# A bound moved behind its exponential, from VectorE to GpSimd, in the time mixing of an RWKV-7 trunk

## The chip, the cores and the metric

The kernel runs on one core of one Trainium2 chip. The metric is the device time of one execution in microseconds. The engines are named as the profile names them: PE is TensorE's matmuls and PEld its weight loads, DVE is VectorE, ACT is ScalarE, POOL is GpSimd, SP is SyncE, which issues most DMAs. An engine works through its own queue in order; the engines wait for each other by semaphores.

## The reference, cut to what matters

Two layers work on 256 tokens of width 2048. The first layer is RWKV-7 time mixing and an MLP, the second chunked attention and an MLP. The change is in the time mixing, where two low-rank products give a decay and a rate for each token and channel:

```python
w_log = -jax.nn.softplus(-(w0 + jnp.tanh(xw @ w1) @ w2)) - 0.5
a = jax.nn.sigmoid(a0 + (xa @ a1) @ a2)
...
decay = jnp.exp(-jnp.exp(heads(w_log)))
...
S = (S * w_t[:, :, None, :] + sa[..., None] * (kk_t * a_t)[:, :, None, :]
     + v_t[..., None] * k_t[:, :, None, :])
```

With z the sum in the inner brackets, softplus(-z) is ln(1 + exp(-z)), and the sigmoid of z is exp(-ln(1 + exp(-z))). Both halves share the inner exponential and the logarithm.

## The kernel before, in words

The 32 heads are worked as 16 pairs of 64 + 64 channels, one pair to the 128 partitions, with the 256 tokens along the free dimension. The recurrence is replaced by four chunks of 64 tokens: inside a chunk a triangular matrix is inverted by products, and the state is carried from chunk to chunk.

The work on a pair is a generator of 36 steps in three parts: early (8 steps), invert (12) and late (16). A new pair begins every 8 slots, so up to five pairs are under way at a time. When one pair takes its first early step, the pair ahead takes its first invert step and the one before that the ninth invert step.

A slot is put together thus. First come the small products of the pairs under way, inversions before the rest, in an order that the program fixes on PE. Behind them come twelve dense products of a projection (w_k, then w_r, for the pair that begins next), which fill PE while the other engines prepare the following slot. Weight halves are made at given places of the eight slots: wH by ACT (L420), wL by DVE (L423). DVE also adds up the modulation, one 128x1024 block at a time (L501). The order of a queue on ACT, DVE and POOL is otherwise set by a planner when the program is built. It goes by program order and by what it reckons to be ready first. A change of an instruction or of its engine can therefore move other instructions too.

These are the steps that the change and the prediction speak of:

- early, step 1: the two low-rank products z on PE (L157, L158) into one PSUM bank of 512 columns (two such banks, "ms", go round), the bound (L162, DVE), the exponential (L163, ACT), and the split square of k (L145, L148 on ACT, L149 on DVE).
- early, step 2: the logarithm (L167) and the two outer exponentials (L168, L169) on ACT.
- early, steps 3 to 6: the running sum of the log decay (L174, DVE), its exponentials (L176, L178, ACT), and on POOL pc (L180), km (L188), bh (L190, L201) and kh (L205).
- invert, step 1: ar (L246, DVE) and the diagonal blocks da and co (L252, L254, ACT) out of one product. Then POOL makes u (L255, L256) and the masks al (L259).
- invert, further steps: u is turned by DVE (L266, the tile tt), PE multiplies it with al (L135), ACT copies the product (xs, L278 and L283), PE multiplies again, DVE adds to u (L289). In the ninth invert step and behind it POOL copies u into uf (L284).
- late: chunk by chunk on PE (L588), with ACT's g and sa (L324, L330), DVE's zs (L341, L343) and ACT's zd (L349); at the end the variance's pair of activations (L358, L359).

The tile that takes the bound is one [128, 512] buffer, "s2", used by every pair in turn: the decay's half is sw, the rate's half is a.

Of the kernel before, what the change touches and what calls it, by code (L numbers as in the profile page):

```python
# [14 lines left out]
AF = mybir.ActivationFunctionType  # L15
ALU = mybir.AluOpType
# [61 lines left out]
class Pair:  # L78
# [13 lines left out]
    def s(self, name="s", bufs=6):  # L92
        return self.b.pw.tile([P, T], F32, tag=name, bufs=bufs, name=name)
# [4 lines left out]
    @staticmethod  # L98
    def ch(t):
        return t.rearrange("p (c t) -> p c t", t=C)  # L100
# [51 lines left out]
    def early(self):  # L152
        b, nc, j, v, s, ch = self.b, self.b.nc, self.j, self.v, self.s, self.ch
        pw, vec, cst, e01 = b.pw, b.vec, b.cst, self.e01
        lw = self.lw
        z = b.psm()
        nc.tensor.matmul(z[:, 0:T], lw[:, 0, :], self.tw, start=True, stop=True)  # L157
        nc.tensor.matmul(z[:, T:2 * T], lw[:, 1, :], self.ta, start=True, stop=True)  # L158

        both = pw.tile([P, 2 * T], F32, tag="s2", bufs=1, name="s2")  # L160
        sw, a = both[:, 0:T], both[:, T:2 * T]
        nc.vector.tensor_scalar(out=both, in0=z, scalar1=-80.0, scalar2=None, op0=ALU.max)  # L162
        nc.scalar.activation(both, both, AF.Exp, scale=-1.0)  # L163
        k = self.k
        sq = self.parts(k, None, AF.Square, vec("k_k", j))
        yield
        nc.scalar.activation(both, both, AF.Ln, bias=b.col(C_ONE))  # L167
        nc.scalar.activation(sw, sw, AF.Exp, scale=-1.0, bias=b.col(C_MHALF))  # L168
        nc.scalar.activation(a, a, AF.Exp, scale=-1.0)  # L169
        yield  # L170
        pss = b.psm()[:, :T]
        self.head_sums(pss, sq)
        cum = s()
        nc.vector.tensor_tensor_scan(out=cum, data0=cst("reset"), data1=sw, initial=0.0, op0=ALU.mult, op1=ALU.add)  # L174
        e0, e1 = e01[:, :, 0:C], e01[:, :, 1:C + 1]
        nc.scalar.activation(e1, ch(cum), AF.Exp, scale=-1.0)  # L176
        e2 = s()
        nc.scalar.activation(e2, cum, AF.Exp)  # L178
        self.pc = pw.tile([P, 4, 1], F32, tag="pc", bufs=4, name="pc")
        nc.gpsimd.tensor_copy(self.pc, e01[:, :, C:C + 1])  # L180
        yield
        rs, ss, rr = s(), s(), s()
        nc.vector.tensor_scalar(out=ss, in0=pss, scalar1=1e-24, scalar2=None, op0=ALU.max)
        nc.scalar.activation(rs, ss, AF.Ln)
        nc.scalar.activation(rs, rs, AF.Exp, scale=-0.5)
        nc.scalar.activation(rr, rs, AF.Square)
        km = s()
        nc.gpsimd.tensor_scalar(out=km, in0=a, scalar1=-1.0, scalar2=vec("k_a", j), op0=ALU.add, op1=ALU.mult)  # L188
        self.bh, self.kh = s("bh", 1), s("kh", 2)
        nc.gpsimd.tensor_tensor(out=self.bh, in0=a, in1=e2, op=ALU.mult)  # L190
        yield
        nc.vector.scalar_tensor_tensor(out=rr, in0=rr, scalar=-0.5, in1=ss, op0=ALU.mult, op1=ALU.mult)
        nc.vector.scalar_tensor_tensor(out=rs, in0=rr, scalar=1.5, in1=rs, op0=ALU.add, op1=ALU.mult)
        kk = s()
        nc.vector.scalar_tensor_tensor(out=kk, in0=k, scalar=vec("k_k", j), in1=rs, op0=ALU.mult, op1=ALU.mult)
        nc.vector.scalar_tensor_tensor(out=km, in0=km, scalar=1.0, in1=k, op0=ALU.add, op1=ALU.mult)
        yield
        r, kr = self.r, self.big("kr", 4)
        self.kr = kr
        nc.vector.tensor_tensor(out=kr[:, :, 0:C], in0=ch(kk), in1=e0, op=ALU.mult)  # L200
        nc.gpsimd.tensor_tensor(out=self.bh, in0=self.bh, in1=kk, op=ALU.mult)  # L201
        nc.vector.tensor_tensor(out=kr[:, :, C:P], in0=ch(r), in1=e1, op=ALU.mult)
        rkp = s()
        nc.vector.scalar_tensor_tensor(out=rkp, in0=r, scalar=vec("r_k", j), in1=km, op0=ALU.mult, op1=ALU.mult)
        nc.gpsimd.tensor_tensor(out=self.kh, in0=km, in1=e2, op=ALU.mult)  # L205
        rkp = self.parts(rkp, rkp)
        yield

        self.vp = pw.tile([P, 4, C], F32, tag="vp", bufs=4, name="vp")
        pt = self.two()  # L210
        yield self.each(pt, 0, C, lambda c: ch(v)[:, c, :], lambda c: cst("cen"))
        nc.scalar.copy(self.even_odd(self.vp), self.by_chunk(pt, 2, C))
        yield
        pt = self.two()
        bk = self.bk = b.pw.tile([P, 3, 2, C], F32, tag="bk", bufs=4, name="bk")
        yield [p for i, t in enumerate((self.bh, self.kh))
               for p in self.each(pt, 2 * C * i, C, lambda c: ch(t)[:, c, :], lambda c: self.b.cst("eye"), 3)]
        for e in range(2):
            p_ = pt[:, e, 0:4 * C].rearrange("p (a i k) -> p i a k", a=2, k=C)
            nc.scalar.copy(bk[:, e::2], p_[:, 0:2 - e])  # L220
        pbn = b.psm()[:, :T]
        self.head_sums(pbn, rkp)
        nc.vector.tensor_tensor(out=v, in0=pbn, in1=v, op=ALU.mult)
        yield
# [145 lines left out]
class Body:  # L370
# [9 lines left out]
    def cst(self, name, rows=slice(None)):  # L380
        o, n = CST_AT[name]
        return self.csts[rows, o:o + n]
# [5 lines left out]
    def vec(self, name, kt=None):  # L388
        i = VI[name]
        return self.vecs[:, i, :] if kt is None else self.vecs[:, i, kt:kt + 1]  # L390
# [1031 lines left out]
```

## Time and profile before

| | us |
|---|---|
| median of 3 runs | 2601.4 (2600.03 to 2603.03) |
| profiled execution | 2600.04 |
| its span | 2598.3 |
| stretch in which pairs 2 to 15 are worked | about 225 to 575 |

The page of the profile gives the busy time of each engine over the span. A view by stretches of time gives the same for a part of it. A view of the waits lists who waited for whom. The timeline lists instructions in order of time: start in us from the span's start, duration in us, engine, line, operation, what it writes and reads, its shape, how often; in square brackets stands the idle time of the engine in front of it and who ended it. The ends of matmuls are modelled, so a busy PE may still hold short gaps.

### The profile page before, as it was taken

The numbers are of one execution on the slowest core, as the hardware profiler recorded it, in microseconds if no ns is written. First come the engines' busy times: TensorE is split into PE (matmuls) and PEld (weight loads), VectorE is DVE, ScalarE is ACT, GpSimd is POOL, SyncE is SP. The second block draws the span as 40 slices with busy tenths as digits, with TensorE's granted clock in tenths as the row PEclk, the third lists the DMA queues.
The fourth block names the chain that finished last, engine by engine and source line by source line (L and its number), as shares of the span: only waits on it lengthen the run. The fifth ranks groups of instructions, "written<-read, shape, count | busy, mean of one in ns | idle before, by whom it ended". The sixth has DMA issues, their size and how long they took to land.

```text
span 2598.3 us, 58875 instructions
## 1 busy us (share of the span) xinstructions
PE 2541.2 (98%) x24018; PEld 2225.7 (86%) x24018; DVE 2075.9 (80%) x3020; ACT 1371.4 (53%) x2535; POOL 229.2 (9%) x336
## 2 busy tenths in 40 slices
PE   6998999999999999999999999999999999999998
PEld 4788888888998888888888988887998888888887
DVE  6888889998899888888889898899896555556555
ACT  3346666674565364464455554565564463553554
POOL 0003333331200000000001000000100000000001
PEclk9999999999999999999999999999999999999999
DMA  9966666667869899888898688887676555555553
GB/s 364 366 232 195 216 213 223 212 217 222 307 220 338 322 329 343 326 323 316 313 323 291 201 305 304 309 277 261 233 258 212 187 187 188 187 188 191 187 187 130
DMA packets 207119, 662.65 MB, mean 255 GB/s; under 512 B 21248, under 2 KB 53632, under 8 KB 206848
## 3 DMA queue, kind: packets, MB, share of 16 engines
q1 hardware_dynamic: 205072, 657.02, 73.1%
q8 instruction: 188, 3.08, 0.5%
q10 hardware_dynamic: 1776, 1.87, 0.2%
q14 instruction: 83, 0.68, 0.1%
HBM read 656.71 MB, written 2.10 MB: 254 GB/s over the span
## 4 chain that ended last, share of the span: by engine, by line
PE 80%; DVE 10%; issue 4%; ACT 3%; DMA 2%; POOL 1%; SPq 0%; ACTq 0%; DVEq 0%; POOLq 0%
PE pj L454 43%; PE pj L456 21%; DVE acc L501 3%; PE pj L443 3%; PE pj L444 2%; PE pj L445 2%; DVE wL L423 2%; PE lt L588 1%; PE o L443 1%; DMA rada<-w_ada 1%; ACT wH L420 1%; PE o L444 1%; PE o L445 1%; ACT da L252 1%; PE pT L1310 0%
## 5 line engine op out<-in xcount | busy, mean ns | idle before, releaser
L423 DVE TENSOR_TENSOR wL<-raw,wH 128x1024 fp32r<-128x1024 f32 x771 | 946.6, 1229 | 336.7 <-ACT wH L420 334.1
L420 ACT CAST wH<-raw 128x1024 fp32r<-128x1024 f32 x771 | 805.3, 1045 | 729.6 <-PE pj L454 579.0
L454 PE MATMUL pj<-aHL,wH 128*128 128x512 f32 x2816 | 894.0, 398 | 1.2 <-DVE x L1135 1.1
L454 PE MATMUL pj<-hHL,wH 128*128 128x512 f32 x2048 | 644.2, 396 | 0.0
L456 PEld LDWEIGHTS pj<-aHL,wL 128*128 128x128 f32 x2816 | 531.7, 189 | 124.2 <-issue 0.3
L456 PE MATMUL pj<-aHL,wL 128*128 128x256 f32 x2816 | 563.0, 281 | 0.0
L501 DVE SCALAR_TENSOR_TENSOR acc<-rada,ct,acc 128x1024 f32<-128x1024 f32 x360 | 462.7, 1285 | 9.5 <-DMA rada<-w_ada 9.1
L456 PEld LDWEIGHTS pj<-hHL,wL 128*128 128x128 f32 x2048 | 384.2, 188 | 91.1 <-DVE wL L423 0.7
L454 PEld LDWEIGHTS pj<-aHL,wH 128*128 128x128 f32 x2816 | 431.6, 189 | 8.9 <-issue 8.5
L456 PE MATMUL pj<-hHL,wL 128*128 128x256 f32 x2048 | 402.0, 278 | 0.3 <-DVE wL L423 0.3
L454 PEld LDWEIGHTS pj<-hHL,wH 128*128 128x128 f32 x2048 | 312.0, 189 | 1.3 <-DVE hHL L1181 1.1
L443 PE MATMUL pj<-aHL,wH 128*128 128x256 f32 (+1 forms) x896 | 263.4, 294 | 1.5 <-ACT r L1018 1.4
L444 PE MATMUL pj<-aHL,wH 128*128 128x256 f32 (+1 forms) x896 | 253.7, 283 | 0.0
L445 PE MATMUL pj<-aHL,wL 128*128 128x256 f32 (+1 forms) x896 | 252.5, 282 | 0.0
L620 POOL TENSOR_TENSOR ss<-ss,sq 128x256 f32<-128x256 f32 x56 | 52.7, 942 | 1579.7 <-ACT sq L619 1532.1
L443 PEld LDWEIGHTS pj<-aHL,wH 128*128 128x128 f32 x896 | 169.8, 189 | 6.1 <-ACT r L1018 2.1
L1206 DVE SCALAR_TENSOR_TENSOR x<-pj,mod,x 128x256 f32<-128x256 f32 x256 | 123.4, 482 | 64.1 <-PE pj L456 61.1
L444 PEld LDWEIGHTS pj<-aHL,wH 128*128 128x128 f32 x896 | 169.6, 189 | 0.8
L445 PEld LDWEIGHTS pj<-aHL,wL 128*128 128x128 f32 x896 | 170.1, 190 | 0.2
L1178 ACT ACTIVATE t<-t 128x256 f32<-128x256 f32 x112 | 46.8, 418 | 119.6 <-DVE t L1150 119.6
L1181 DVE TENSOR_TENSOR hHL<-t,hHL 128x256 fp32r<-128x256 f32 x128 | 53.9, 421 | 1.8 <-ACT t L1180 1.1
L1180 ACT ACTIVATE t<-t 128x256 f32<-128x256 f32 x128 | 53.3, 416 | 3.3
(270 smaller groups left out, 2757.9 us busy)
## 6 DMA issues: line engine op xcount, KB each, us to landing
rada<-w_ada SPq DMA_DIRECT2D x320, 512.0 KB, 5.2
raw<-w_up SPq DMA_DIRECT2D x256, 512.0 KB, 4.1
raw<-w_down SPq DMA_DIRECT2D x256, 512.0 KB, 3.8
rada<-w_ada_kv SPq DMA_DIRECT2D x64, 512.0 KB, 6.3
rawa<-w_ada SPq DMA_DIRECT2D x32, 512.0 KB, 9.1
rawa<-w_ada_t SPq DMA_DIRECT2D x32, 512.0 KB, 8.6
raw<-w_k SPq DMA_DIRECT2D x32, 512.0 KB, 5.0
raw<-w_r SPq DMA_DIRECT2D x32, 512.0 KB, 4.0
```

The source lines that it names most:

```text
L420: nc.scalar.copy(Hf, raw)
L423: eng.tensor_tensor(out=Lf, in0=raw, in1=Hf, op=ALU.subtract)
L443: nc.tensor.matmul(ps, H[:, i, :], a(kt)[:, 0, :], start=(first and kt == 0), stop=False)
L444: nc.tensor.matmul(ps, H[:, i, :], a(kt)[:, 1, :], start=False, stop=False)
L445: ins = nc.tensor.matmul(ps, L[:, i, :], a(kt)[:, 0, :], start=False, stop=(last and kt == KT - 1))
L454: nc.tensor.matmul(ps, w[kt // HK][0][:, kt % HK, :], a(kt), start=(kt == 0), stop=False)
L456: ins = nc.tensor.matmul(ps[:, 0, :], w[kt // HK][1][:, kt % HK, :], a(kt)[:, 0, :], start=False, stop=(kt == KT - 1))
L501: nc.vector.scalar_tensor_tensor(out=self.acc, in0=raw, scalar=ck, in1=self.acc, op0=ALU.mult, op1=ALU.add)
L620: (eng or nc.gpsimd).tensor_tensor(out=self.ss, in0=self.ss, in1=sq, op=ALU.add)
L1180: nc.scalar.activation(t, t, AF.Square)
L1181: nc.vector.tensor_tensor(out=h[:, 1, :], in0=t, in1=h[:, 0, :], op=ALU.subtract)
L1206: nc.vector.scalar_tensor_tensor(out=x, in0=ps[:, i, :], scalar=self.mods[(layer, 5)][:, n:n + 1], in1=x, op0=ALU.mult, op1=ALU.add)
```

## The change

The maximum with -80 by DVE, which read the product out of PSUM and wrote the tile, is removed. ACT's exponential now reads PSUM itself and writes the tile. Behind it POOL takes the minimum with exp(80) in place, and the logarithm reads what POOL left. The value that the logarithm sees is the same up to rounding: exp(-max(z, -80)) is min(exp(-z), exp(80)).

```diff
         both = pw.tile([P, 2 * T], F32, tag="s2", bufs=1, name="s2")
         sw, a = both[:, 0:T], both[:, T:2 * T]
-        nc.vector.tensor_scalar(out=both, in0=z, scalar1=-80.0, scalar2=None, op0=ALU.max)
-        nc.scalar.activation(both, both, AF.Exp, scale=-1.0)
+        nc.scalar.activation(both, z, AF.Exp, scale=-1.0)
+        nc.gpsimd.tensor_scalar(out=both, in0=both, scalar1=math.exp(80.0), scalar2=None, op0=ALU.min)
         k = self.k
         sq = self.parts(k, None, AF.Square, vec("k_k", j))
         yield
```

## The prediction

> **What bounds the kernel now.** I read the page first, then the busy times of the stretch in which the sixteen head pairs are worked (225 to 575 us), then the waits there, then one pair in order of time.
>
> ```profile
> span 2598.3 us, 58875 instructions
> ...
> PE 2541.2 (98%) x24018; PEld 2225.7 (86%) x24018; DVE 2075.9 (80%) x3020; ACT 1371.4 (53%) x2535; POOL 229.2 (9%) x336
> ```
>
> TensorE is busy nearly throughout. The same in the pairs' stretch (start and end, its length, then busy us of PE, PEld, DVE, ACT, POOL, the granted clock, the DMA share and GB/s):
>
> ```profile
> 225.00:575.00 350.00, 337.96 (x8183) 305.44 (x8184) 318.38 (x558) 225.02 (x651) 130.13 (x162) 1.00 0.67 217
> ```
>
> PE is at 97% (338.0 of 350), DVE at 91%, ACT at 64%, POOL at 37%, at the full clock. So what is taken from DVE counts only where PE waits for it. The waits from 225 to 600 us (who waits, for whom: us in total, times, longest):
>
> ```profile
> POOL kh L205 <- DVE s L196: 35.7, 15, 3.4
> ...
> DVE tt L266 <- POOL u L256: 7.5, 12, 1.0
> ...
> ACT da L252 <- DVE ar L246: 6.9, 11, 1.1
> ...
> DVE u L289 <- PE iv L135: 4.1, 8, 1.1
> ...
> PE iv L135 <- DVE tt L266: 3.4, 7, 1.2
> PE iv L135 <- issue: 2.9, 5, 0.8
> ...
> PE iv L135 <- POOL al L259: 2.3, 3, 0.9
> ```
>
> PE's three longest sums are 3.4, 2.9 and 2.3 us, 8.6 us together, or 0.3% of the span. That is about all this stretch has to give. Now one pair, the eighth, around the changed lines (start, duration, engine, line, operation):
>
> ```profile
> 369.22 1.04 ACT L420 CAST wH<-raw 128x1024 fp32r<-128x1024 f32 x1
> 369.49 0.59 PE L158 MATMUL ms<-ta,lw 128*128 128x256 f32 x2
> ...
> 370.24 0.42 DVE L246 TENSOR_TENSOR ar<-gr,csts 128x256 f32<-128x256 f32 x1
> ...
> 370.75 0.26 ACT L252 COPY da<-gr 32x128 f32<-32x128 f32 x1 [0.48 <-DVE ar L246]
> ...
> 370.91 0.68 DVE L162 TENSOR_SCALAR s<-ms 128x512 f32<-128x512 f32 x1
> ...
> 371.96 0.29 DVE L289 TENSOR_TENSOR u<-u,iv 128x128 f32<-128x128 f32 x1 [0.37 <-PE iv L135]
> ...
> 372.18 0.63 ACT L163 ACTIVATE s<-s 128x512 f32<-128x512 f32 x1
> ...
> 372.23 0.41 POOL L255 TENSOR_TENSOR u<-da,csts 128x128 f32<-128x128 f32 x1 [14.10 <-ACT da L252]
> ...
> 372.72 0.41 POOL L256 TENSOR_TENSOR u<-u,csts 128x128 f32<-128x128 f32 x1
> ...
> 372.84 0.73 ACT L167 ACTIVATE s<-s,csts 128x512 f32<-128x512 f32 x1
> ...
> 373.08 1.11 POOL L259 TENSOR_TENSOR al<-da,csts 128x512 f32<-128x512 f32 x1
> ...
> 373.16 0.32 DVE L266 STREAM_TRANSPOSE tt<-u 128x128 f32<-128x128 f32 x1 [0.57 <-POOL u L256]
> ...
> 373.56 1.72 DVE L423 TENSOR_TENSOR wL<-raw,wH 128x1024 fp32r<-128x1024 f32 x1
> ...
> 374.13 2.52 POOL L284 COPY uf<-u 32x128 f32<-32x128 f32 x2
> ...
> 374.43 0.23 PE L135 MATMUL iv<-tt,al 32*32 32x32 f32 x3
> ```
>
> Two things are to be seen. The urgent chain is ar (L246), da (ACT), u and al (POOL), then PE's product of tt and al: al ends at 374.19 and PE starts on it at 374.43, 0.24 us of slack. And the removed bound (L162) lies beside this chain, in front of a gap: DVE then waits 0.37 us for PE and 0.57 us for POOL.
>
> **The change, part by part.** These are the rows for the prices (min, median, max in ns):
>
> ```profile
> L162 DVE TENSOR_SCALAR s<-ms x16: 683/684/692, 203.5 to 575.9; 128x512 f32<-128x512 f32 x16
> L163 ACT ACTIVATE s<-s x16: 614/632/635, 204.3 to 577.2; 128x512 f32<-128x512 f32 x16
> L188 POOL TENSOR_SCALAR s<-s,vecs x16: 476/646/1749, 210.0 to 584.9; 128x256 f32<-128x256 f32 x16
> L180 POOL COPY pc<-e x16: 186/644/1059, 209.0 to 583.8; 128x4 f32<-128x4 f32 x16
> L259 POOL TENSOR_TENSOR al<-da,csts x16: 1087/1107/1121, 224.4 to 603.8; 128x512 f32<-128x512 f32 x16
> L145 ACT ACTIVATE sq<-s x16: 416/417/419, 215.5 to 593.8; 128x256 fp32r<-128x256 f32 x16
> L145 ACT ACTIVATE sq<-lt x16: 383/384/387, 288.2 to 656.9; 128x256 fp32r<-128x256 f32 x16
> ```
>
> *Removed from DVE:* 16 x 0.684 = 10.9 us. No DMA moves. Behind L162 come DVE's waits for PE (4.1 us in all) and for POOL's u (7.5 us), 11.6 us together, as much as is removed: most of it only lengthens them. Bounds: nothing, if the gap swallows all, and 3.4 us, if PE's waits for the transposes (L266) all go. I take 1.5 us gained, near the middle, because two transposes run per step and only one of them can come earlier; the other waits for POOL.
>
> *ScalarE reads PSUM:* the same 512 columns. L145 takes 417 ns out of SBUF and 384 out of PSUM, so I expect 0.63 - 0.03 = 0.60 us, 16 x 0.03 = 0.5 us in all, off the urgent chain: nothing. The bank of the product is released when the exponential ends instead of the maximum; if ScalarE keeps its place that is 372.81 instead of 371.59, 1.2 us later, and the other "ms" bank serves meanwhile. Without that cover PE would wait up to 1.2 us per pair, 19 us; I take nothing, as PE's listed waits show none on an "ms" bank being full.
>
> *Place of the exponential:* it no longer needs L162, so it is ready when L158 ends (about 370.1), and ScalarE is idle from 370.26 to 370.75, before da. This idle time is 6.9 us over 11 pairs. The exponential can go there, or stay behind da. In front, 16 x 0.60 = 9.6 us stand against 6.9, so da comes up to 2.7 us late in sum, some 0.17 us per pair, against 0.24 us of slack of al: bounds 0 and 2.7 us lost. I take 0.5, nearer to nothing because of that slack. It costs the whole 0.60 us per pair, 9.6, where ScalarE has no idle time there.
>
> *Added on POOL:* no row shows a one-input operation on 512 columns there. Undisturbed, L188 takes 476 ns for 256 columns and L180 186 for 4, so (476 - 186) / 252 = 1.15 ns a column and 476 + 256 x 1.15 = 771 ns (estimate). Below it stands 476, the half size; above it 1107, two inputs of 512 columns; L188's slowest (1749) adds 1.27 for a disturbed one: 2.04. I take 0.8 us; POOL is at 37%, and with 16 x 0.8 = 12.8 us in the stretch stays near 41%.
>
> *The new wait:* the logarithm (L167) waits for POOL. Behind it on ScalarE stand both exponentials, the variance's pair (L358, L359) and the copies xs and g that PE needs. With the exponential ahead of da it ends near 370.9, the minimum by 371.7, before da ends at 372.15: POOL is free then (idle 14.10 us before L255) and the logarithm can start when it does now. Behind da, the minimum follows al (374.19) and ends at 375.0; the logarithm is 2.1 us later, and the planner can put other work of ScalarE ahead of it. On POOL the copies uf (L284) and km (L188) come up to 0.8 us later; behind km POOL waits 35.7 / 15 = 2.4 us per pair for DVE (L205), which covers it. I take nothing, bounds under the rivals.
>
> *Sum:* -1.5 + 0.5 = -1.0 us on the profiled execution's 2600.0 us (the span of 2598.3 and 1.7 around it), 2599.0. The median of the three runs shown is 1.4 us above the profiled time, so I forecast 2600.4.
>
> *The shared read path.* POOL and DVE disturb each other here: L423 took 1.72 us beside al and uf, against its mean in the whole kernel:
>
> ```profile
> L423 DVE TENSOR_TENSOR wL<-raw,wH 128x1024 fp32r<-128x1024 f32 x771 | 946.6, 1229 | 336.7 <-ACT wH L420 334.1
> ```
>
> That is 0.49 us more. The Trainium skill ("SBUF — State Buffer", section "Who interferes with whom") says that a VectorE instruction with two SBUF inputs and a GpSimd instruction that reads SBUF contend for one read interface, and that the later one blocks fully. By that rule the work moved to POOL would take from DVE as much as it frees. In this trace the delay is part of the POOL work beside it, so the rule is half borne out; I take it as the second rival below.
>
> **The rivals.**
>
> 1. *The relief reaches PE.* Both transposes come earlier, and the exponential leaves ScalarE's chain. For it speaks the chain of waits one pair later, which runs through it to the variance's exponential:
>
> ```profile
> 397.64 0.64 ACT s L163
> ...
> 400.65 0.42 ACT sl L359
> ```
>
> PE's waits for the transposes (3.4) and al (2.3) and half of those put down to issue (1.45) go: 7.2 us gained, 2594.2. Against it: al is on POOL and is not sped up.
>
> 2. *DVE gets nothing.* The minimum holds up L423 or the modulation's L501 (both read two SBUF inputs) for its 0.77 us: 16 x 0.77 = 12.3 us against 10.9 freed. The gain of 1.5 drops out and 1.4 us of DVE work are added: +1.4 + 0.5 = 1.9, 2603.3. For it L423's 1.72; against it DVE's gap at 371.6 to 371.96, where the minimum would lie.
>
> 3. *The minimum gets in front of al.* POOL works in order; a minimum between L256 and L259 makes al late by 0.8 to 1.1 us, less 0.24 of slack: 0.56 to 0.86 us of PE per pair, times 15 (the first pair has no second inversion beside it) 8.4 to 12.9, middle 10.7: 2612.1, slower. It decides as soon as the minimum begins behind 372.2 and ahead of al. Against it: al stands earlier in the program and is ready when u is.
>
> 4. *ScalarE stalls.* The logarithm waits 2.1 us behind al with the order of ScalarE's queue kept. The next copy that PE needs:
>
> ```profile
> 376.18 0.27 ACT L278 COPY xs<-iv 128x128 f32<-128x128 f32 x1
> ```
>
> ```profile
> 377.19 0.23 PE L135 MATMUL iv<-u,xs 32*32 32x32 f32 x3
> ```
>
> It ends at 376.45, 0.74 us ahead of PE; 2.1 - 0.74 = 1.36 us per pair, times 13, is 17.7 us: 2619.1. Against it: the planner sets the queue's order, and the exponential fits ahead of da.
>
> If the planner moved nothing but left the exponential behind da with other work filling the wait, the change would in effect do nothing; that lies inside the first forecast.
>
> **How the numbers follow.** The forecast (2600.4) has a chance of 0.36, rival 1 0.29, rival 2 0.09, rival 3 0.12, rival 4 0.14. I count 0.2%, 5.2 us, as what a measurement here tells from no change. Rival 1 is faster (0.29), the forecast and rival 2 are the same (0.45), rivals 3 and 4 slower (0.26). The range reaches below rival 1 to 2592, as all 8.6 us of PE's three waits could go (2592.8), and above to the middle of rival 3 (2612): outside lie rival 4 and half of rival 3's upper part. The likeliest case's own range, from -3.4 to +2.7 us, is 2598 to 2604.
>
> **What would show it.** Right: L162 gone from DVE; the exponential's start ahead of da or next to it; a POOL row of 0.7 to 1.1 us for the minimum; DVE's waits for L289 and u grown by most of 10.9 us; al's end unmoved against PE's product; PE busy within 2 us in the stretch. Rival 1: PE's wait for the transposes near nothing. Rival 2: the L423 beside the minimum at 1.7 us or more while others stay near 1229 ns, and DVE no less busy in the stretch than 318.4 us. Rival 3: PE's wait for al well above 2.3 us. Rival 4: ScalarE waiting for POOL ahead of L167 by 2 us. The forecast is wrong if PE's idle time in the stretch changes by over 5 us.

## The result, and the profile after

The changed kernel is slower: a median of 2647.9 us in 5 runs (2645.9 to 2648.3) against 2601.4, a ratio of 1.0169 [1.0157, 1.018] (the brackets hold a 95% interval), or 44 us by the ratio; the two medians are 46.5 us apart, the spans of the two profiled executions 46.1. The forecast was 2600.4. In the profiled execution (2646.2 us) two lines of the page show nearly the same instructions, busy a little longer:

```profile
span 2644.4 us, 58878 instructions
...
PE 2557.9 (97%) x24018; PEld 2239.8 (85%) x24018; DVE 2071.0 (78%) x3004; ACT 1369.8 (52%) x2535; POOL 236.2 (9%) x352
```

DVE has its 16 instructions fewer and POOL its 16 more. The loss lies in the pairs' stretch. The view by stretches, with the columns of the row of before (busy us of PE, PEld, DVE, ACT, POOL, granted clock, DMA share, GB/s):

```profile
225.00:575.00 350.00, 316.53 (x7255) 284.79 (x7257) 280.82 (x489) 200.56 (x581) 123.41 (x162) 0.95 0.60 197
```

PE is idle 33.5 us of the 350, where it was idle 12.0, and its granted clock is 0.95, where it was 1.00. In the same time it does 7255 products instead of 8183. The two changed lines (duration min, median and max in ns, then the first and the last start in us):

```profile
L162 ACT ACTIVATE s<-ms x16: 596/597/602, 203.1 to 618.2; 128x512 f32<-128x512 f32 x16
...
L163 POOL TENSOR_SCALAR s<-s x16: 1486/2339/2377, 203.8 to 621.1; 128x512 f32<-128x512 f32 x16
```

L162 is now the exponential and L163 the minimum. The exponential of the first and of the last pair are 415.1 us apart; before they were 372.9 (204.3 to 577.2). So 15 intervals grew by 42.2 us, 2.8 us each, which is nearly the whole of the 46.1 us between the two spans. The exponential costs 0.60 us, as worked out; the minimum costs 2.34 and not 0.77. Who waits for whom from 225 to 640 us (us in total, times, longest):

```profile
ACT s L167 <- POOL s L163: 54.7, 15, 4.3
...
PE ms L135 <- ACT xs L283: 23.0, 11, 2.8
...
DVE u L289 <- PE iv L135: 12.5, 14, 1.7
...
PE ms L523 <- ACT xs L283: 4.3, 2, 2.2
```

The first row leads to the second and the fourth: the logarithm (L167) waits 54.7 us for the minimum, and PE waits 23.0 + 4.3 = 27.3 us in 13 pairs for a copy (xs, L283) that ACT has standing behind the logarithm. None of the three was among the waits of this stretch before. The eighth pair in order of time:

```profile
382.71 0.59 PE L158 MATMUL ms<-ta,lw 128*128 128x256 f32 x2
...
383.91 0.26 ACT L252 COPY da<-gr 32x128 f32<-32x128 f32 x1 [0.42 <-DVE ar L246]
...
385.34 0.60 ACT L162 ACTIVATE s<-ms 128x512 f32<-128x512 f32 x1
...
386.26 1.12 POOL L259 TENSOR_TENSOR al<-da,csts 128x512 f32<-128x512 f32 x1
...
386.73 1.72 DVE L423 TENSOR_TENSOR wL<-raw,wH 128x1024 fp32r<-128x1024 f32 x1
...
387.46 2.34 POOL L163 TENSOR_SCALAR s<-s 128x512 f32<-128x512 f32 x1
...
388.38 1.62 DVE L501 SCALAR_TENSOR_TENSOR acc<-rada,ct,acc 128x1024 f32<-128x1024 f32 x1
...
389.84 0.72 ACT L167 ACTIVATE s<-s,csts 128x512 f32<-128x512 f32 x1 [3.90 <-POOL s L163]
...
391.89 0.53 ACT L283 COPY xs<-ms 32x128 f32<-32x128 f32 x2
...
392.46 0.44 PE L135 MATMUL ms<-u,xs 32*32 32x32 f32 x16 [2.13 <-ACT xs L283]
```

To compare with before, put both kernels on PE's time: L158 began at 369.49 and now begins at 382.71, 13.22 us later. The exponential stayed behind da, where it was (372.18 + 13.22 = 385.40, now 385.34). al ends at 387.38, or 374.16 on the old time; it was 374.19. The minimum begins directly behind al and ends at 389.80. The logarithm, at 372.84 + 13.22 = 386.06 before, now starts at 389.84, 3.78 us late. ACT makes up part of that, because the copy xs now ends 2.58 us behind the logarithm's start (392.42 - 389.84). It was 3.32 us before, when PE began its product 0.87 us behind the end of xs (376.16 to 377.03):

```profile
375.63 0.53 ACT L283 COPY xs<-ms 32x128 f32<-32x128 f32 x2
...
377.03 0.34 PE L135 MATMUL ms<-u,xs 32*32 32x32 f32 x10
```

Now PE's product (L135) waits 2.13 us for xs.

A second loss follows the wait. The clock granted to PE behind it, in the view by stretches for PE alone (start and end, length, busy us, granted clock, DMA share, GB/s):

```profile
390.00:392.00 2.00, 0.33 (x3) 1.00 0.95 293
...
393.00:394.00 1.00, 0.80 (x36) 0.59 0.04 16
394.00:395.00 1.00, 1.00 (x13) 0.50 0.00 0
395.00:396.00 1.00, 1.00 (x3) 0.50 0.00 0
396.00:397.00 1.00, 1.00 (x6) 0.70 0.72 147
397.00:398.00 1.00, 1.00 (x10) 1.00 0.85 348
```

PE is idle, resumes at 392.46, and from 393 to 397 us the clock misses 0.41 + 0.50 + 0.50 + 0.30 = 1.71 us of its full rate, which is 3.42 us at one half. One group of four dense products, in the timeline of PE, now and in the same pair before:

```profile
394.61 2.07 PE L364 MATMUL lt<-tg,lg 128*128 128x256 f32 x4
```

```profile
378.16 1.13 PE L364 MATMUL lt<-tg,lg 128*128 128x256 f32 x4
```

The four take 2.07 us instead of 1.13. The Trainium skill ("TensorE: Matmul & The Clock Gate", Part 1: The HAM clock gate) says that the clock has two levels, half and full, and that it is decided by free-running windows of 3.41 us. The level of 0.50 and the length of 3.42 us agree. The Trainium skill's rule on the same page (section "HAM oscillation — how this bites in real kernels"), to have no idle gaps over some 3.4 us, would have passed a wait of 2.13 us; here a stretch at half clock followed it.

Not every wait has such a stretch behind it. Of the 13 waits for xs eight do, of 1.58 to 2.45 us; five do not, of 1.42 to 2.75 us (behind the longest, which ended at 626.43, the clock stayed at 1.00). What decides between them was not tested.

Over the whole span, PE's row of the page splits the loss. PE's idle time grew from 57.1 us (2598.3 - 2541.2) to 86.5 (2644.4 - 2557.9), by 29.4 us; the 27.3 us of waiting for xs are nearly as much. The same 24018 products kept PE busy 16.7 us longer (2557.9 - 2541.2). Together that is the 46.1 us between the spans. The view of the cores gives the mean granted clock, after and before:

```profile
core 0: 2644.4 us, clock 0.987
```

```profile
core 0: 2598.3 us, clock 0.996
```

2644.4 x 0.013 = 34.4 us of clock are missing after, 2598.3 x 0.004 = 10.4 before: 24 us more, give or take 2.6 for the rounding. That is a bound on what the clock cost, because clock that is missing while PE stands idle costs no time; the busy row says 16.7. So nearly two thirds of the loss are waiting, and some third is products that take longer, with the half clock behind the waits as the cause that the trace shows. The ends of matmuls are modelled, so the split is rough.

### The profile page after: what moved, and what is told of

Same layout as the page of the kernel before. It is cut to its first block, busy times and chain, and to the rows that moved or that the text cites. A ratio compares the mean times of both kernels' runs of the same rounds, so it can differ in the third digit from the quotient of the medians.

```text
span 2644.4 us, 58878 instructions
## 1 busy us (share of the span) xinstructions
PE 2557.9 (97%) x24018; PEld 2239.8 (85%) x24018; DVE 2071.0 (78%) x3004; ACT 1369.8 (52%) x2535; POOL 236.2 (9%) x352
## 4 chain that ended last, share of the span: by engine, by line
PE 79%; DVE 8%; ACT 4%; issue 4%; POOL 3%; DMA 1%; ACTq 0%; DVEq 0%; SPq 0%; POOLq 0%
PE pj L454 42%; PE pj L456 21%; PE pj L443 3%; PE pj L444 2%; PE pj L445 2%; DVE wL L423 2%; DVE acc L501 2%; POOL s L163 1%; PE lt L588 1%; ACT wH L420 1%; PE lt L364 1%; PE o L443 1%; POOL al L259 1%; ACT da L252 1%; PE o L444 1%
## 5 line engine op out<-in xcount | busy, mean ns | idle before, releaser
L423 DVE TENSOR_TENSOR wL<-raw,wH 128x1024 fp32r<-128x1024 f32 x771 | 947.1, 1230 | 335.4 <-ACT wH L420 333.3
L501 DVE SCALAR_TENSOR_TENSOR acc<-rada,ct,acc 128x1024 f32<-128x1024 f32 x360 | 466.1, 1295 | 6.7 <-DMA rada<-w_ada 6.3
L443 PE MATMUL pj<-aHL,wH 128*128 128x256 f32 (+1 forms) x896 | 267.5, 299 | 1.8 <-ACT r L1018 1.7
L444 PE MATMUL pj<-aHL,wH 128*128 128x256 f32 (+1 forms) x896 | 256.0, 286 | 0.0
L1178 ACT ACTIVATE t<-t 128x256 f32<-128x256 f32 x112 | 46.9, 419 | 119.5 <-DVE t L1150 119.5
L1179 ACT ACTIVATE hHL<-t 128x256 fp32r<-128x256 f32 x128 | 53.0, 414 | 4.1 <-DVE t L666 3.1
```

The costliest lines, as they stand in the source:

```text
L423: eng.tensor_tensor(out=Lf, in0=raw, in1=Hf, op=ALU.subtract)
L443: nc.tensor.matmul(ps, H[:, i, :], a(kt)[:, 0, :], start=(first and kt == 0), stop=False)
L444: nc.tensor.matmul(ps, H[:, i, :], a(kt)[:, 1, :], start=False, stop=False)
L501: nc.vector.scalar_tensor_tensor(out=self.acc, in0=raw, scalar=ck, in1=self.acc, op0=ALU.mult, op1=ALU.add)
L1179: nc.scalar.activation(h[:, 0, :], t, AF.Square)
```

## The experiments

All ratios are against the kernel before, timed on the same chip. L-numbers are those of the changed kernel, except where an experiment says otherwise.

**The minimum left out.**

```diff
         nc.scalar.activation(both, z, AF.Exp, scale=-1.0)
-        nc.gpsimd.tensor_scalar(out=both, in0=both, scalar1=math.exp(80.0), scalar2=None, op0=ALU.min)
```

> The changed kernel without the minimum: ScalarE's exponential still reads PSUM, and nothing stands between it and the logarithm (the bound is left out of the computation). Theory 'the wait': the 46.5 us come from ScalarE standing at the logarithm for GpSimd's minimum (3.90 us in the eighth pair, PE then 2.13 us late for xs), so this kernel runs in 2593 to 2603 us. Rival 'PSUM': the later release of the bank and the exponential's new place are what costs; then about 2640 us. Rival 'order': the planner's new order of the queues costs by itself; then anywhere from 2615 to 2645 us.

2601.9 us, ratio 0.999 [0.998, 1.0]. The stretch:

```profile
225.00:575.00 350.00, 339.09 (x8157) 306.15 (x8158) 310.28 (x547) 223.04 (x649) 129.66 (x161) 1.00 0.68 218
```

PE is busy 339.1 us (338.0 before) at full clock. The read out of PSUM and the work taken from DVE together are worth 0.1%, at most 0.2%. The loss belongs to the minimum and to what waits for it.

**Both bounds: the kernel before, with the minimum added.** The edit is shown against the changed kernel.

```diff
+        nc.vector.tensor_scalar(out=both, in0=z, scalar1=-80.0, scalar2=None, op0=ALU.max)
-        nc.scalar.activation(both, z, AF.Exp, scale=-1.0)
+        nc.scalar.activation(both, both, AF.Exp, scale=-1.0)
         nc.gpsimd.tensor_scalar(out=both, in0=both, scalar1=math.exp(80.0), scalar2=None, op0=ALU.min)
```

> The kernel before, with VectorE's maximum kept, and GpSimd's minimum added behind the exponential (it changes no value). Theory 'the wait': slow as the changed kernel, 2640 to 2655 us, the exponential being some 0.6 us later at most. Rival 'PSUM': 2600 to 2606 us, as VectorE still empties the bank. If the wait explains only half, about 2625 us.

2651.7 us, ratio 1.0188 [1.0171, 1.0204].

```profile
ACT s L167 <- POOL s L163: 57.5, 15, 4.0
...
PE ms L135 <- ACT xs L283: 24.2, 12, 2.9
```

The same two waits, and the same loss. That DVE keeps its maximum matters by no more than the 0.2% between this ratio and that of the change, whose intervals overlap.

**The minimum by DVE, at the same place.**

```diff
-        nc.gpsimd.tensor_scalar(out=both, in0=both, scalar1=math.exp(80.0), scalar2=None, op0=ALU.min)
+        nc.vector.tensor_scalar(out=both, in0=both, scalar1=math.exp(80.0), scalar2=None, op0=ALU.min)
```

> The changed kernel with the minimum by VectorE, in place, where GpSimd had it. A [128, 512] operation on VectorE out of SBUF should take 0.4 to 0.7 us (L162 took 0.684 out of PSUM) and not stand behind the masks al. Theory 'the wait': the logarithm waits under 1.5 us and PE about 0.5 us per pair, 2602 to 2615 us. Rival 'any round trip to another engine costs as much': about 2640 us. Rival 'GpSimd slows VectorE': this load on the shared reads is gone, 2598 to 2604 us.

2608.0 us, ratio 1.0018 [1.0008, 1.0027].

```profile
L163 DVE TENSOR_SCALAR s<-s x16: 417/608/1083, 204.2 to 584.1; 128x512 f32<-128x512 f32 x16
```

```profile
ACT s L167 <- DVE s L163: 9.5, 13, 1.4
```

A step between the exponential and the logarithm need not cost much: DVE does it in 0.61 us and is not held up by al, so ACT waits 9.5 us instead of 54.7. It is the place behind al and POOL's duration that cost the rest.

**The logarithm one step later, behind ACT's copies.** In this kernel the three activations (L167 to L169) are issued a step later, and the planner may not put them ahead of the copies that end the step before. POOL's minimum stays.

```diff
-        sq = self.parts(k, None, AF.Square, vec("k_k", j))
-        yield
-        nc.scalar.activation(both, both, AF.Ln, bias=b.col(C_ONE))
...
+        sq = self.parts(k, None, AF.Square, vec("k_k", j)); yield; yield; pss = b.psm()[:, :T]; self.head_sums(pss, sq)
+        with b.behind():
+            nc.scalar.activation(both, both, AF.Ln, bias=b.col(C_ONE))
...
```

> The changed kernel with GpSimd's minimum, but the logarithm and both outer exponentials a step later and behind the copies xs and g of that slot in ScalarE's queue, so that nothing that PE needs stands behind the wait. Theory 'the wait holds up what is queued behind it': PE's waits for xs (27.3 us in all) go, the pair's own chain is some 3 us later and covered by its slack, 2600 to 2615 us. Rival 'the pair's own chain (logarithm, running sum, exponentials) is what is late': no better than the changed kernel, 2645 us or more.

2611.9 us, ratio 1.0029 [1.0018, 1.004].

```profile
ACT s L167 <- POOL s L163: 10.0, 13, 1.4
...
PE pj L443 <- ACT r L1018: 5.6, 10, 0.8
```

The minimum takes as long as in the changed kernel (median 2.34 us), and PE works in the same order, as does POOL but for the copies uf of one pair. On ACT the copies xs now stand ahead of the logarithm; the planner has moved other work too, on ACT and on DVE behind it (the running sum comes later, for one). 36 of the 44 us are gone: (1.0169 - 1.0029) x 2601 = 36.4. So most of the loss was carried by what stood behind the waiting logarithm in ACT's queue, and not by POOL's load. PE's waits for L283 are off the list. A smaller wait, for the copy r (L1018), has come instead.

**Product, exponential and minimum one slot earlier.** Here the minimum has a slot of time before the logarithm needs it. Pairs begin one slot earlier, and the weight work keeps its slots.

```diff
-    EARLY, INVERT, LATE = 8, 12, 16
+    EARLY, INVERT, LATE = 9, 12, 16
...
-        k = self.k
+        yield; k = self.k
...
-    LEAD = 4
+    LEAD = 5
...
-                    if (slot + lead) % S in (1, 3, 6, 7):
+                    if (slot + lead - 1) % S in (1, 3, 6, 7):
...
```

> The changed kernel with the low-rank products, the exponential out of PSUM and GpSimd's minimum one slot (about 3 us) earlier than the square of k and the logarithm, which stay where they were. The early part has 9 steps for 8, and a pair begins one slot sooner. Theory 'the wait': the minimum (2.34 us beside VectorE's weight halves) is done before the logarithm is due; ScalarE's wait for it falls from 54.7 us to under 10, and the time is 2596 to 2606 us. Rival 'GpSimd's load on the shared reads costs VectorE its gain': the wait is gone but the time is 2606 to 2620 us. Rival 'the pair's own chain': it begins as before, so this rival too expects 2600 us.

2627.4 us, ratio 1.0085 [1.0069, 1.0101]: above what was expected.

```profile
ACT s L167 <- POOL s L163: 26.9, 14, 2.4
...
PE pj L443 <- ACT k L1018: 15.9, 13, 1.7
```

The logarithm still waits 26.9 us. The planner, with its order free again, put it ahead of the copy of k, and PE waits 15.9 us for that copy. The blocking has moved to another copy.

The same move with the kernel before, whose maximum stays on DVE, tells what the move itself costs:

```diff
...
         nc.scalar.activation(both, both, AF.Exp, scale=-1.0)
-        k = self.k
+        yield; k = self.k
...
-    LEAD = 4
+    LEAD = 5
...
```

> The kernel before, VectorE's maximum kept, with the low-rank products, the maximum and the exponential one slot earlier. It holds the move of the run beside it without the change. If the move is worth nothing by itself: 2599 to 2605 us. If it takes the exponential off ScalarE's crowded place behind da, up to 5 us faster, 2595. The difference between this and the run beside it is what GpSimd's minimum is worth once nothing waits for it: by the forecast 1 to 3 us in favour of GpSimd, by the rival of the shared reads 2 to 6 us against it.

2612.4 us, ratio 1.0028 [1.0016, 1.004]: slower than was expected.

```profile
PE lt L588 <- ACT sa L330: 13.8, 11, 1.5
```

The move costs 0.28% without any minimum on POOL, with a new wait of PE for sa. So of the 0.85% about 0.57% belong to the minimum at its new place, if the two costs add up. The third kernel of this group is the move with the logarithm held behind the copies, as above:

```diff
...
         yield; k = self.k
...
+        with b.behind():
+            nc.scalar.activation(both, both, AF.Ln, bias=b.col(C_ONE)); nc.scalar.activation(sw, sw, AF.Exp, scale=-1.0, bias=b.col(C_MHALF))
+            nc.scalar.activation(a, a, AF.Exp, scale=-1.0)
...
```

> The low-rank products, the exponential and GpSimd's minimum one slot earlier as before, and now the logarithm held behind the copies of its own slot in ScalarE's queue. In the run one slot earlier the planner had put the logarithm too early, in front of the copy of k, which PE's next projection waits for (15.9 us). Theory 'what is queued behind the wait': PE's wait for k goes and the time is 2600 to 2612 us. Rival 'GpSimd's load or the move itself': 2620 to 2630 us as without it.

2618.0 us (2609.4 to 2623.0 in 4 runs), ratio 1.005 [1.0031, 1.0069]: between the two times that were expected.

```profile
PE iv L135 <- POOL al L259: 10.5, 13, 2.5
...
POOL u L255 <- ACT da L252: 54.7, 16, 13.6
```

```profile
L256 POOL TENSOR_TENSOR u<-u,csts x16: 401/887/902, 226.9 to 623.5; 128x128 f32<-128x128 f32 x16
```

PE no longer waits for the copy of k. Now it waits 10.5 us for al. The minimum stands ahead of u and al in POOL's queue, but it is over before they are due: POOL then stands idle until da comes (54.7 us in 16 times). What takes longer is the second half of u (L256), 0.89 us instead of 0.41 in the changed kernel. In the ninth pair DVE's running sum (L174), which waits for the late logarithm's exponential, begins at 409.08 and L256 at 409.09, so that the two run side by side. Each of the three kernels that moved the logarithm or the minimum ended with another wait of PE (for r, for k, for al). Whether a further order would be free of them was not tested.

**A price list.** To see what one POOL instruction of each kind costs here, the kernel before was given five extra instructions per pair on a scratch tile (16 each). They stand in this order in lines 376 to 380, t is the scratch tile and v a column of scalars. The kernel's time of 2668 us, expected within 5 us of before, says nothing on the change.

```diff
-        yield
+        yield; self.probe(vec("k_a", j))
...
+    nc.gpsimd.tensor_scalar(out=t, in0=t, scalar1=math.exp(80.0), scalar2=None, op0=ALU.min)
+    nc.gpsimd.tensor_scalar(out=t, in0=t, scalar1=1.0, scalar2=None, op0=ALU.mult)
+    nc.gpsimd.tensor_scalar(out=t, in0=t, scalar1=0.0, scalar2=v, op0=ALU.add, op1=ALU.mult)
+    nc.gpsimd.tensor_scalar(out=t[:, 0:T], in0=t[:, 0:T], scalar1=math.exp(80.0), scalar2=None, op0=ALU.min)
+    nc.gpsimd.tensor_scalar(out=t[:, 0:T], in0=t[:, 0:T], scalar1=0.0, scalar2=v, op0=ALU.add, op1=ALU.mult)
```

> The kernel before with five operations on a scratch tile in GpSimd's idle time behind kh, for each of the sixteen pairs: minimum with a constant on 512 columns, product with a constant on 512, sum and product with a [128, 1] operand on 512, minimum on 256, sum and product on 256. The undisturbed price is the shortest of the sixteen. Theory 'an operation with a constant is dear on GpSimd': 1.49 us for the minimum and the product on 512 columns, 0.77 for sum and product. Rival 'the price is by columns': all three on 512 columns 1.4 to 1.5 us and those on 256 half of it, the 476 ns of L188 being a recorded span that is too short. Rival 'minimum alone is dear': 1.49 for the minimum, 0.77 for the other two. The time of the kernel: within 5 us of before.

```profile
L376 POOL TENSOR_SCALAR scr<-scr x16: 1483/1484/1526, 205.5 to 304.0; 128x512 f32<-128x512 f32 x16
...
L377 POOL TENSOR_SCALAR scr<-scr x16: 1492/1493/1802, 207.1 to 305.6; 128x512 f32<-128x512 f32 x16
...
L378 POOL TENSOR_SCALAR scr<-scr,vecs x16: 691/692/2828, 209.0 to 307.2; 128x512 f32<-128x512 f32 x16
...
L379 POOL TENSOR_SCALAR scr<-scr x16: 848/849/1934, 210.8 to 308.0; 128x256 f32<-128x256 f32 x16
...
L380 POOL TENSOR_SCALAR scr<-scr,vecs x16: 474/478/1512, 211.7 to 309.3; 128x256 f32<-128x256 f32 x16
```

L380 is the form of km (474 ns at its shortest, L188 476), from which the prediction took its price. On 512 columns this form takes 0.69 us, near the estimate of 0.77. But a minimum against a constant takes 1.48 us, and so does a product with a constant: 2.5 ns a column ((1484 - 849) / 256) against 0.8 ((692 - 478) / 256). The form with two operations, the second with a column of scalars, is the cheap one.

**A minimum in a form hoped to be cheap.** The minimum and then a product with a column of ones, in one instruction; the value is the same and the queues' orders are those of the changed kernel.

```diff
-        nc.gpsimd.tensor_scalar(out=both, in0=both, scalar1=math.exp(80.0), scalar2=None, op0=ALU.min)
+        nc.gpsimd.tensor_scalar(out=both, in0=both, scalar1=math.exp(80.0), scalar2=b.col(C_ONE), op0=ALU.min, op1=ALU.mult)
```

> The changed kernel with the minimum in the form that the price list shows to be cheap for sum and product: a second operation, a product with a [128, 1] column of ones, behind the minimum (no value changes). Every engine's queue keeps its order. The theory has two terms, the place (behind al) and the price (1.49 us undisturbed, 2.34 beside VectorE's weight half). If this form costs 0.69 us undisturbed, the minimum ends 0.8 to 1.65 us sooner, ScalarE waits 2.3 to 3.1 us in place of 3.90, and the time is 2610 to 2630 us: the place alone explains the first half of the loss and the price the second. If the price is of the minimum in any form: 2648 us. If the place costs nothing: 2602 us.

2659.8 us, ratio 1.0215 [1.0201, 1.0229]. The form is dearer, not cheaper:

```profile
L163 POOL TENSOR_SCALAR s<-s,csts x16: 1997/2845/3139, 204.8 to 633.1; 128x512 f32<-128x512 f32 x16
```

```profile
ACT s L167 <- POOL s L163: 61.9, 15, 4.4
...
PE ms L135 <- ACT xs L283: 26.6, 10, 3.3
```

So the second operation does not make it cheap. The same form with the logarithm held behind the copies:

```diff
-        nc.gpsimd.tensor_scalar(out=both, in0=both, scalar1=math.exp(80.0), scalar2=None, op0=ALU.min)
+        nc.gpsimd.tensor_scalar(out=both, in0=both, scalar1=math.exp(80.0), scalar2=b.col(C_ONE), op0=ALU.min, op1=ALU.mult)
...
+        with b.behind():
+            nc.scalar.activation(both, both, AF.Ln, bias=b.col(C_ONE))
...
```

> The cheap form of the minimum together with the logarithm a step later behind the copies xs and g. The run with the later logarithm alone lost 0.29% (2609 to 2614 us) with ScalarE still waiting 10.0 us for GpSimd. If that rest is the minimum's price: 2600 to 2607 us. If it is the later chain of the pair (k, r and the running sum): 2609 to 2614 us as without it.

2617.2 us, ratio 1.0048 [1.0034, 1.0062]: above both times that were expected.

```profile
ACT s L167 <- POOL s L163: 18.4, 13, 2.3
```

A step of 2.85 us costs 0.48% there, and one of 2.34 us 0.29%. The intervals of the two ratios overlap, so that the length of the minimum is felt there too is likely, but not shown.

**More forms.** A second list on a scratch tile, in the same way (2679 us, which says nothing on the change), lines 376 to 379:

```diff
+    nc.gpsimd.tensor_scalar(out=t, in0=t, scalar1=math.exp(80.0), scalar2=b.col(C_ONE), op0=ALU.min, op1=ALU.mult)
+    nc.gpsimd.tensor_scalar(out=t, in0=t, scalar1=b.col(C_ONE), scalar2=None, op0=ALU.min)
+    nc.gpsimd.tensor_scalar(out=t, in0=t, scalar1=math.exp(80.0), scalar2=0.0, op0=ALU.min, op1=ALU.add)
+    nc.gpsimd.tensor_copy(t[:, 0:T], t[:, T:2 * T])
```

> The kernel before with four operations on a scratch tile on GpSimd for each pair: minimum with a constant and product with a [128, 1] column, minimum with a [128, 1] column alone, minimum with a constant and sum with a constant (each on 512 columns), and a copy of 256 columns. Read are the shortest of sixteen alone; the kernel's own time says nothing, as these operations stand in front of its own work (the other price list ran in 2668 us). If two operations in one instruction are what is cheap: 0.69, 1.49, 0.69 us. If the [128, 1] operand is what is cheap: 0.69, 0.69, 1.49 us.

```profile
L376 POOL TENSOR_SCALAR scr<-scr,csts x16: 1999/2000/3297, 203.9 to 310.6; 128x512 f32<-128x512 f32 x16
...
L377 POOL TENSOR_SCALAR scr<-scr,csts x16: 1558/1559/1807, 206.0 to 312.7; 128x512 f32<-128x512 f32 x16
...
L378 POOL TENSOR_SCALAR scr<-scr x16: 1924/1924/2292, 207.7 to 314.4; 128x512 f32<-128x512 f32 x16
```

Every form with a minimum takes 1.48 us or more. Of the forms tried, only the sum-and-product is cheap.

**A cheap instruction in the minimum's place.** The sum with zero and the product with a column of ones, in the place of the minimum.

```diff
-        nc.gpsimd.tensor_scalar(out=both, in0=both, scalar1=math.exp(80.0), scalar2=None, op0=ALU.min)
+        nc.gpsimd.tensor_scalar(out=both, in0=both, scalar1=0.0, scalar2=b.col(C_ONE), op0=ALU.add, op1=ALU.mult)
```

> The changed kernel with a sum with zero and a product with a [128, 1] column of ones in the minimum's place on GpSimd (the bound is left out of the computation). The order of every queue is that of the changed kernel. This form took 0.69 us undisturbed where the minimum took 1.48; beside VectorE's weight half it should take 0.7 to 1.6. It is the price that the prediction assumed (0.77), at the place that its fourth rival assumed (behind al). From the two runs that differ in the price alone (2.34 us at 1.0169, 2.85 us at 1.0215, 23 us of time for each us of price) 1.5 us gives 2628 us and 0.7 us 2609. By the fourth rival's own sum it is 2619 us. If the place alone cost everything, 2645 us; if nothing, 2602 us.

2635.3 us, ratio 1.0109 [1.0092, 1.0126].

```profile
L163 POOL TENSOR_SCALAR s<-s,csts x16: 907/1658/1922, 203.6 to 606.8; 128x512 f32<-128x512 f32 x16
```

```profile
ACT s L167 <- POOL s L163: 43.6, 14, 3.5
...
PE ms L135 <- ACT xs L283: 14.8, 11, 2.0
```

Between al and the logarithm even the cheapest form costs 28 us. It takes 1.66 us there, beside L423 and L501, against 0.69 on the list. With the queues' orders alike, three lengths of the POOL step now stand side by side:

| POOL step | its median, us | ratio | us over before | granted clock, 215 to 665 us |
|---|---|---|---|---|
| sum and product | 1.66 | 1.0109 | 28.4 | 0.96 |
| minimum (the change) | 2.34 | 1.0169 | 44.0 | 0.95 |
| minimum and product | 2.85 | 1.0215 | 56.0 | 0.92 |

The us over before are the ratio's part above 1 times the median of before; the clock of the kernel before in that stretch is 0.99. From row to row, 0.68 us more cost 15.6, and 0.51 us more cost 12.0: 23 us of time for each us of the step, give or take some 5 by the intervals of the first and the last ratio. In 16 pairs that is 1.4 us for 1 us. The wait alone would give at most 1. The clock column falls with it, which fits the half-clock stretches as the rest.

## Why the prediction was wrong

The prediction would be wrong, it said, if PE's idle time in the stretch changed by over 5 us; it changed by 21.4.

*What failed first: the place of the exponential, and "I take nothing" for the new wait.* The forecast rested on the exponential going ahead of da, or on other ACT work filling the wait. The planner did that in one pair only, the third. Elsewhere it left the exponential behind da and, in most pairs, the logarithm directly behind the exponential. This is the mechanism of rival 4, which had been given 0.14. The words "the planner can put other work of ScalarE ahead of it" were a possibility without a row behind it: the queue's order is fixed when the program is built, from what the planner reckons to be ready first, and here it did not move xs. The runs with the logarithm held back (1.0029) and with DVE's minimum (1.0018) show that an order or an engine without that block was there to be had.

*What failed second: the price of 0.77 us.* The two-point estimate used L188, a sum and product, for a minimum. The undisturbed minimum takes 1.48 us, above the upper bound of 1.107 that the text gave for it, and 2.34 at its place, above the 2.04 given for a disturbed one. A row of the same engine and the same number of inputs was not a row of the same operation.

*What was not foreseen: the clock.* No term held that PE's clock drops to 0.50 for 3.4 us behind a wait of 2 us. Products that take longer make up 16.7 of the 46.1 us; the missing clock would allow up to some 24.

*Rival 4's own sum.* It said 2619.1: the logarithm 2.1 us late, less 0.74 of slack, times 13. The mechanism was right, with 13 pairs in which PE waits for xs; the sizes were not. The eighth pair goes as follows: 3.78 us late instead of 2.1 (the longer minimum), ACT makes up 0.74 (the copy ended 3.32 us behind the logarithm's start before, 376.16 - 372.84, and ends 2.58 behind it now), and the slack of xs L283 was 0.87 (377.03 - 376.16): 3.78 - 0.74 - 0.87 = 2.17, against 2.13 measured. Thirteen times 2.13 is 27.7, against 27.3 measured in the 13 pairs. The 16.7 us of longer products come on top, and no term of the rival held them.

*Rival 3* (the minimum in front of al) occurred in the third pair, where the exponential ran ahead of da: PE waited 1.20 us for al there. In the others the minimum followed al, as predicted for that place. In the kernel with the move and the logarithm held al is late in 13 places, but for another reason, as shown there.

*The parts that held.* The PSUM read makes the exponential 0.60 us instead of 0.63. The relief of DVE is swallowed by its waits: L289's wait for PE, 4.1 us before, is 12.5 in the changed kernel and 11.4 in the one without the minimum, which gains 0.1%, at most 0.2%. *Rival 2* holds in part. In the eighth pair the minimum began while L423 had 0.99 us to go (387.46 to 388.45), and took 0.86 us longer than undisturbed, 2.34 instead of 1.48: it gave way for most of that time. L501 began during the minimum and lay 1.42 us beside it, but took only 1.62 us (its mean in the whole kernel after is 1.295), so DVE did not give way in the same manner. As a price of the change this hardly counts, since PE waits little for DVE: its longest such wait in the stretch is 2.9 us in all, for L183.

*Open.* What is left of the kernel with the logarithm held (0.29%) has PE's 5.6 us for the copy r, other short waits and some clock in it; no run separates them. Why one slot earlier costs 0.28% without any POOL step was not followed beyond PE's wait for sa. No kernel with a bound in it beat the one before; a minimum on DVE with the logarithm held back was not run.

## What to carry to other kernels

Before a step is put between two instructions of one engine on another engine, ask what stands behind the second in its in-order queue and how much slack that has; the step's own load on a 37%-busy engine said nothing here. Take the price from a row of the same operation in the same form, and from a disturbed one, if it will run beside something. A wait of TensorE can cost more than its length, as here: read the granted clock behind it.

## What the runs showed of the hardware that was not expected

- On POOL the price of a one-input instruction on 128x512 fp32 depends on the operation: minimum or product with a constant 1.48 to 1.49 us, minimum against a column 1.56, minimum and sum 1.92, minimum and product 2.00, sum and product with a column 0.69. The Trainium skill ("GPSIMD Engine Reference", section 4.1 Engine selection) calls one-input elementwise work there roughly line-rate. The minimum does not agree: DVE's shortest took 417 ns, POOL's 1483.
- TensorE's clock fell to 0.50 for about 3.4 us, or twice that, behind eight of the 13 waits for xs (1.58 to 2.45 us, with small 32x32 products around them), and not behind the other five (1.42 to 2.75 us).
- POOL's step took about 0.9 us longer, whatever its form, where it began while DVE's L423 still had some 1 us to go: 1.48 to 2.34, 2.00 to 2.85, 0.69 to 1.66. In the tenth pair of the kernel with the logarithm behind the copies it began ahead of L423 and lay 0.88 us beside it: there it took 1.49 us and L423 1.18.
